# Two of seven half products read an operand's high and low part in one 512-column pass

## The chip, the cores and the metric

The kernel runs on one core of one Trainium2 chip. The metric is the device time of one execution in microseconds; times are given as the median of several runs. TensorE (PE) does the matmuls, with its weight loads shown as a row of their own (PEld); VectorE (DVE) and ScalarE (ACT) do the elementwise work; SyncE (SP) and GpSimd (POOL) issue the transfers.

## The reference

One layer of an encoder over 512 positions and 1024 channels, in fp32:

```python
x = x + 0.5 * swiglu(rms_norm(x, ffn1_norm), ffn1_w_gate, ffn1_w_up, ffn1_w_down)   # inner width 2752
h = rms_norm(x, mix_norm); u = h @ w_in
...                                              # a Fourier mixer and grouped attention, and w_out
x = x + concat([f_out, a_out]) @ w_out
x = x + 0.5 * swiglu(rms_norm(x, ffn2_norm), ffn2_w_gate, ffn2_w_up, ffn2_w_down)
return rms_norm(x, final_norm)

def swiglu(h, w_gate, w_up, w_down):
    return (silu(h @ w_gate) * (h @ w_up)) @ w_down
```

The change touches `h @ w_gate` and `h @ w_up` of both feed-forward layers.

## The kernel before

**Numbers in two parts.** TensorE works on `float32r` operands here, so each operand is held as a high part (the rounded value) and a low part (what the rounding left). A product of two operands is three matmuls that add up in one PSUM bank: high weights with high values, high weights with low values, low weights with high values. ScalarE makes a high part by a copy with a cast; VectorE makes the low part by a subtraction (`lows`, L128).

**The feed-forward layers.** The inner width is cut into 21 blocks of 128 columns (and a rest of 64). A function `ffn` runs each layer in groups of blocks: the gate and up products of a group, then the down product (`dn`) that adds this group's share to all eight output blocks. The first group of each layer is done in the plain way. From there on 35 blocks, called j (17 in the first layer, 18 in the second), are done in `seven(js, done)`, in three calls per layer: six, six and five blocks in the first layer, and six, six and six in the second. Each call is one long stretch of matmuls on TensorE, and a `dn` stretch follows it.

**Seven products in place of eight.** For a block j, the gate and up weights (1024 by 128 each) and the values (1024 by 512) form a 2 by 2 product of halves, done by Winograd's scheme with seven half products. Each half product has a weight half (`a11`, `a12`, `s1`, `s2`, `s4`, `s3`, `a22`: 512 by 128, four pieces of 128 by 128) and a half of the values (`b11`, `b21`, `t1`, `t2`, `b22`, `t3`, `t4`: 512 by 256, held in the tile `rt`). `multiply` runs it as 4 pieces times 3 matmuls of 256 columns, each into the first half of a 512-column bank. So a block has 84 passes, and a call of `seven` with six blocks has 72 passes for each block and 12 more, the `a22` product, for each block but the last; the last block's `a22` product comes a little later, between two `dn` passes.

**Which bank, and who reads it.** `step(j, w, n)` is one product and what follows. n = 0 (`a11`) writes bank r, which ScalarE copies to `p1`; n = 1 (`a12`) writes a bank of its own (named p in the profile), and VectorE adds it to `p1` into the second half of `g`; n = 3 (`s1`) writes bank q, copied to `p5`; n = 4 (`s2`) adds to r, copied to `u2`; n = 5 (`s4`) adds to q, and VectorE adds q and `u2` into the first half of `g`, which then gets its Silu on ScalarE; n = 6 (`s3`) adds to r, is copied to `u` and gets `p5`; n = 9 (`a22`, after `a12` of the next block) adds to r and ends the block. A copy has to be done before the next product adds to the same bank: `s4` waits for the copy `p5`, `s3` for the copy `u2`.

**Order.** TensorE and SyncE run in the written order. VectorE and ScalarE run each in an order that the tile scheduler works out when the program is built. `prepare(j)` makes the weight parts of the next block while the present one is multiplied.

**One pass in two pieces.** `parts_of(n)` cuts the pass with number 1 of each call of `seven` into 64 and 192 columns (`CUT = 1, P // 2`); every other pass is one piece. `product` (the plain way) has a form that reads the values in the order that `turned` gives: four columns out of each sixteen, four times; the `dn` passes are of this form, 512 columns each.

Of the kernel before, what the change touches and what calls it, by code (L numbers as in the profile page):

```python
# [13 lines left out]
P = 128  # L14
# [72 lines left out]
def encoder(ctx, tc, A, out):  # L87
# [19 lines left out]
    def bank(name):  # L107
        return pp.tile([P, S], F32, tag="bank", name=name)
# [173 lines left out]
    def ffn(norm, after, wgu, wd, wdt, groups, opening, closing):  # L282
# [6 lines left out]
        with tc.tile_pool(name=f"act{n_}", bufs=1) as ap, tc.tile_pool(name=f"sums{n_}", bufs=2) as sp:  # L289
            room(ap, 128)  # L290
            acts = ap.tile([P, PLACES * 2 * S + ROOM], F32R, name=f"at{n_}")
            at = acts[:, FRONT + LOWER : FRONT + LOWER + PLACES * 2 * S].rearrange("p (n a b) -> p n a b", a=2, b=S)
            rt = ap.tile([P, 7, 2, KH, HALF], F32R, name=f"rt{n_}")
            wt, raws = [], {}
            free, where = list(range(PLACES)), {}

# [110 lines left out]
            def seven(js, done):  # L407

                done = [done]
                banks = {}  # L410
                count = iter(range(84 * len(js)))

                def multiply(ps, wn, on, w, first):

                    (whi, wlo), (mhi, mlo) = w[wn], (part[on][:, i] for i in range(2))
                    for i in range(KH):
                        ks = slice(i * P, (i + 1) * P)
                        for o, (a, b) in enumerate(((whi, mhi), (whi, mlo), (wlo, mhi))):
                            for t in parts_of(next(count)):
                                nc.tensor.matmul(  # L420
                                    ps[:, t], a[:, ks], b[:, i, t], start=first and i == 0 and o == 0,
                                    stop=i == KH - 1 and o == 2, skip_group_check=not first,
                                )
                    give(*w.get((wn, "slots"), ()))

                def kept(ps, n, j):
                    t = sp.tile([P, HALF], F32, tag=n, name=f"{n}{n_}_{j}")
                    nc.scalar.copy(t, ps)  # L428
                    return t

                def step(j, w, n):
                    b = banks.setdefault(j, {})
                    if n == 0:
                        b["r"] = bank(f"r{n_}_{j}")[:, :HALF]
                        multiply(b["r"], "a11", "b11", w, True)
                        b["p1"] = kept(b["r"], "p1", j)
                    elif n == 1:
                        ps = bank(f"p2{n_}_{j}")[:, :HALF]
                        multiply(ps, "a12", "b21", w, True)
                        b["g"] = tp.tile([P, S], F32, tag="g", name=f"g{n_}_{j}")  # L440
                        nc.vector.tensor_tensor(out=b["g"][:, HALF:], in0=ps, in1=b["p1"], op=ALU.add)
                    elif n == 3:
                        b["q"] = bank(f"q{n_}_{j}")[:, :HALF]
                        multiply(b["q"], "s1", "t1", w, True)
                        b["p5"] = kept(b["q"], "p5", j)
                    elif n == 4:
                        multiply(b["r"], "s2", "t2", w, False)
                        b["u2"] = kept(b["r"], "u2", j)
                    elif n == 5:
                        multiply(b["q"], "s4", "b22", w, False)  # L450
                        nc.vector.tensor_tensor(out=b["g"][:, :HALF], in0=b["q"], in1=b["u2"], op=ALU.add)  # L451
                        nc.scalar.activation(b["g"], b["g"], AF.Silu)  # L452
                    elif n == 6:
                        multiply(b["r"], "s3", "t3", w, False)
                        b["u"] = tp.tile([P, S], F32, tag="u", name=f"u{n_}_{j}")
                        nc.scalar.copy(b["u"][:, :HALF], b["r"])
                        nc.vector.tensor_tensor(
                            out=b["u"][:, :HALF], in0=b["u"][:, :HALF], in1=b["p5"], op=ALU.add
                        )
                    elif n == 9:  # L460
                        multiply(b["r"], "a22", "t4", w, False)
                        u, i = b["u"], place(j)
                        h, l = at[:, i, 0], at[:, i, 1]
                        nc.scalar.copy(u[:, HALF:], b["r"])  # L464
# [1071 lines left out]
```

## Time and profile before

| | |
|---|---|
| Time, median of 3 runs | 821.32 us (820.55 to 821.43) |
| The profiled execution's own time | 820.94 us |
| Its span, first to last instruction | 818.9 us |
| TensorE busy | 812.4 us (99%), 5362 matmuls |
| VectorE busy | 637.5 us (78%), 1003 instructions |
| ScalarE busy | 483.1 us (59%), 810 instructions |
| GpSimd busy | 29.3 us (4%) |
| Transfers | 89.97 MB, 110 GB/s in the mean |

A matmul's row in the profile has a modelled end, and matmuls overlap: the 256-column matmul of `multiply` is listed with 276 ns, but one follows the other much faster. The time that a matmul takes on the engine is therefore read as a pitch: the time of a long row of equal matmuls divided by their number, from the chain of waits or from the starts in the timeline. "Idle before" names what ended an engine's idle time. Line numbers are those of the kernel before.

### The profile page before, as it was taken

The page shows a single profiled execution, that of the slowest core. Times are in us where ns is not written, and L with a number is a line of the kernel's source. Part 1 is how long each engine was busy: PE and PEld are TensorE (multiplying, and loading weights), DVE is VectorE, ACT ScalarE, POOL GpSimd, SP SyncE. Part 2 cuts the span into 40 slices and gives each one's busy share as a digit, 9 for nine tenths or more (in the row PEclk, how much of TensorE's full clock was granted, in tenths as well). Part 3 has the DMA queues.
Part 4 walks back from the last instruction along what each step waited for, and adds up shares of the span by engine and source line. Part 5 has one row for each costly group of instructions (what it writes and reads, how often), then busy time and mean ns, then how long its engine had stood idle before and what let it go on. Part 6 is the DMA issues. An engine that isn't in the chain of part 4 may idle for free.

```text
span 818.9 us, 13611 instructions
## 1 busy us (share of the span) xinstructions
PE 812.4 (99%) x5362; PEld 746.1 (91%) x5362; DVE 637.5 (78%) x1003; ACT 483.1 (59%) x810; POOL 29.3 (4%) x31
## 2 busy tenths in 40 slices
PE   9999999999999999999999999999999999999997
PEld 7889999899989998889998888899989999899987
DVE  7898896479856847799998578999945896479574
ACT  7763674257523735699998448456632673257462
POOL 0110000000000000221000001100000000000001
PEclk9999999999999999999999999999999999999999
DMA  7664322333141223342101234542232322322222
GB/s 258 174 145 179 124 93 77 124 104 142 59 151 71 90 70 116 129 147 66 65 26 52 77 112 127 123 176 108 94 122 114 127 100 69 132 104 97 69 78 103
DMA packets 31568, 89.97 MB, mean 110 GB/s; under 512 B 3728, under 2 KB 9232, under 8 KB 31504
## 3 DMA queue, kind: packets, MB, share of 16 engines
q1 hardware_dynamic: 27776, 82.61, 29.1%
q0 software_dynamic: 3008, 5.51, 3.7%
q10 hardware_dynamic: 720, 0.98, 0.3%
q8 instruction: 42, 0.69, 0.3%
q14 instruction: 22, 0.18, 0.1%
HBM read 84.24 MB, written 2.10 MB: 105 GB/s over the span
## 4 chain that ended last, share of the span: by engine, by line
PE 95%; DVE 2%; ACT 1%; POOL 1%; issue 1%; DMA 0%; POOLq 0%; DVEq 0%; ACTq 0%
PE dn L184 25%; PE r L420 23%; PE q L420 12%; PE gu L184 8%; PE mix L184 6%; PE p L420 6%; PE gu L709 3%; PE mix L1203 2%; PE mix L1169 2%; PE mix L1007 1%; PE mix L1008 1%; PE mix L1009 1%; PE mix L1066 1%; PE mix L1143 1%; PE mix L1144 1%
## 5 line engine op out<-in xcount | busy, mean ns | idle before, releaser
L420 PE MATMUL r<-rt,ring 128*128 128x256 f32 x1686 | 209.2, 276 | 0.0
L184 PE MATMUL dn<-at,ring 128*128 128x512 f32 x900 | 202.5, 380 | 0.0
L420 PEld LDWEIGHTS r<-rt,ring 128*128 128x128 f32 x1686 | 200.3, 188 | 0.8
L184 PEld LDWEIGHTS dn<-at,ring 128*128 128x128 f32 x900 | 168.0, 188 | 28.3
L420 PE MATMUL q<-rt,ring 128*128 128x256 f32 x840 | 106.6, 276 | 0.0
L128 DVE TENSOR_TENSOR ring<-s,ring 128x1024 fp32r<-128x1024 f32 x70 | 85.5, 1221 | 23.8 <-ACT ring L379 20.8
L420 PEld LDWEIGHTS q<-rt,ring 128*128 128x128 f32 x840 | 100.4, 188 | 0.0
L544 DVE SCALAR_TENSOR_TENSOR gx<-dn,gx 128x512 f32<-128x512 f32 x61 | 41.9, 688 | 67.1 <-PE dn L184 67.1
L379 ACT CAST ring<-s 128x1024 fp32r<-128x1024 f32 x70 | 73.5, 1050 | 28.3 <-PE p L420 13.7
L170 ACT CAST ring<-raw_dn 128x768 fp32r<-128x768 f32 (+3 forms) x58 | 45.3, 784 | 72.8 <-PE dn L184 61.9
L128 DVE TENSOR_TENSOR ring<-raw_dn,ring 128x768 fp32r<-128x768 f32 (+3 forms) x58 | 51.5, 892 | 5.7 <-PE r L420 4.4
L420 PE MATMUL p<-rt,ring 128*128 128x256 f32 x420 | 53.3, 276 | 0.0
L128 DVE TENSOR_TENSOR ring<-raw_g,ring 128x1024 fp32r<-128x1024 f32 x35 | 42.7, 1220 | 11.7 <-PE p L420 10.2
L420 PEld LDWEIGHTS p<-rt,ring 128*128 128x128 f32 x420 | 50.2, 188 | 0.0
L184 PE MATMUL gu<-ring 128*128 128x512 f32 x216 | 48.9, 381 | 0.0
L379 ACT CAST ring<-raw_g 128x1024 fp32r<-128x1024 f32 x35 | 36.8, 1051 | 17.2 <-DMA raw_g<-in_wgu 11.5
L184 PEld LDWEIGHTS gu<-ring 128*128 128x128 f32 x216 | 40.4, 188 | 6.9
L428 ACT COPY p<-r 128x256 f32<-128x256 f32 x35 | 12.9, 369 | 44.9 <-PE r L420 44.6
L452 ACT ACTIVATE g<-g 128x512 f32<-128x512 f32 x35 | 22.2, 633 | 23.9 <-DVE g L451 23.6
L388 ACT CAST ring<-raw_u 128x512 fp32r<-128x512 f32 x35 | 21.8, 624 | 16.0 <-PE q L420 15.7
L184 PE MATMUL mix<-near,ring 128*128 128x512 f32 x120 | 28.8, 381 | 0.0
L465 DVE TENSOR_TENSOR u<-g,u 128x512 f32<-128x512 f32 x35 | 24.0, 687 | 6.1 <-ACT u L464 6.0
(266 smaller groups left out, 1314.3 us busy)
## 6 DMA issues: line engine op xcount, KB each, us to landing
raw_g<-in_wgu SPq DMA_DIRECT2D x35, 512.0 KB, 3.8
raw_u<-in_wgu SPq DMA_DIRECT2D x35, 512.0 KB, 4.3
raw_dn<-in_wd SPq DMA_DIRECT2D x40, 384.0 KB, 3.1
raw_gu<-in_wgu SPq DMA_DIRECT2D x12, 512.0 KB, 3.7
raw_o<-in_wo SPq DMA_DIRECT2D x8, 512.0 KB, 3.5
raw_dn<-in_wd SPq DMA_DIRECT2D x8, 448.0 KB, 3.7
raw_wq<-in_wins SPq DMA_DIRECT2D x4, 512.0 KB, 3.5
raw_f<-in_winf SPq DMA_DIRECT2D x4, 512.0 KB, 3.5
```

Source lines behind the costliest of these rows:

```text
L128: nc.vector.tensor_tensor(out=lo, in0=src, in1=asf(hi), op=ALU.subtract)
L170: nc.scalar.copy(hi[:, :n, :], raw[:, :n, :])
L184: nc.tensor.matmul(ps, a, b, start=first and b is mhi and a is whi, stop=last and a is wlo)
L379: nc.scalar.copy(hi, src)
L388: nc.scalar.copy(hi, src)
L420: nc.tensor.matmul(ps[:, t], a[:, ks], b[:, i, t], start=first and i == 0 and o == 0, stop=i == KH - 1 and o == 2, skip_group_check=not first,
L452: nc.scalar.activation(b["g"], b["g"], AF.Silu)
L465: nc.vector.tensor_tensor(out=u, in0=b["g"], in1=u, op=ALU.mult)
L544: nc.vector.scalar_tensor_tensor(out=x[d][:, t], in0=ps[:, t], scalar=0.5, in1=x[d][:, t], op0=ALU.mult, op1=ALU.add)
L709: nc.tensor.matmul(turned(pss[c]), w[:, k % 2, c], turned(m[k]), start=k == 0 and m is hh and w is hi, stop=k == KD - 1 and w is lo,)
L1169: nc.tensor.transpose(pts[n][:, c * P : (c + 1) * P], prob[t, b, c][:, kc * P : (kc + 1) * P], ident)
L1203: nc.tensor.matmul(turned(outs[t, b]), w, turned(p), start=kc == 0 and i == 0, stop=kc == 3 and i == 1)
```

## The change

`a12` and `s4` get a wide form. In `rt`, the high and the low part of a piece now lie side by side (256 and 256 columns). For the two wide products, one 512-column pass in the `turned` order reads both parts with the high weights and writes both halves of the bank: high times high in the first half, high times low in the second. The low weights with the high values are a 256-column pass as before, into the first half. So the bank holds two halves that have to be added: `added` does one more addition of 256 columns on VectorE, for `g`. The other five products keep their three passes of 256 columns. The count of passes starts at 2, so no pass is cut into 64 and 192 columns in `seven` (the one in the last `dn` stretch stays).

```diff
+WIDE = ('a12', 's4')
...
-            rt = ap.tile([P, 7, 2, KH, HALF], F32R, name=f"rt{n_}")
+            rt = ap.tile([P, 7, KH, 2, HALF], F32R, name=f"rt{n_}")
...
-                        h, l = rt[:, c, 0, i], rt[:, c, 1, i]
+                        h, l = rt[:, c, i, 0], rt[:, c, i, 1]
...
-                count = iter(range(84 * len(js)))
+                count = iter(range(2, 84 * len(js)))

                 def multiply(ps, wn, on, w, first):

-                    (whi, wlo), (mhi, mlo) = w[wn], (part[on][:, i] for i in range(2))
+                    whi, wlo = w[wn]
                     for i in range(KH):
-                        ks = slice(i * P, (i + 1) * P)
-                        for o, (a, b) in enumerate(((whi, mhi), (whi, mlo), (wlo, mhi))):
-                            for t in parts_of(next(count)):
-                                nc.tensor.matmul(
-                                    ps[:, t], a[:, ks], b[:, i, t], start=first and i == 0 and o == 0,
-                                    stop=i == KH - 1 and o == 2, skip_group_check=not first,
-                                )
+                        ks, m = slice(i * P, (i + 1) * P), part[on][:, i].rearrange("p a b -> p (a b)")
+                        start, stop = first and i == 0, i == KH - 1
+                        if wn in WIDE:
+                            nc.tensor.matmul(turned(ps), whi[:, ks], turned(m), start=start, stop=False, skip_group_check=True)
+                        else:
+                            for o in range(2):
+                                for t in parts_of(next(count)):
+                                    nc.tensor.matmul(
+                                        ps[:, t], whi[:, ks], m[:, o * HALF :][:, t], start=start and o == 0, stop=False,
+                                        skip_group_check=True,
+                                    )
+                        nc.tensor.matmul(
+                            ps[:, :HALF], wlo[:, ks], m[:, :HALF], start=False, stop=stop, skip_group_check=True
+                        )
...
+                def added(out, ps, other, n):
+                    nc.vector.tensor_tensor(out=out, in0=ps[:, :HALF], in1=other, op=ALU.add)
+                    if n in WIDE:
+                        nc.vector.tensor_tensor(out=out, in0=ps[:, HALF:], in1=out, op=ALU.add)
...
                     elif n == 1:
-                        ps = bank(f"p2{n_}_{j}")[:, :HALF]
+                        ps = bank(f"p2{n_}_{j}")
                         multiply(ps, "a12", "b21", w, True)
                         b["g"] = tp.tile([P, S], F32, tag="g", name=f"g{n_}_{j}")
-                        nc.vector.tensor_tensor(out=b["g"][:, HALF:], in0=ps, in1=b["p1"], op=ALU.add)
+                        added(b["g"][:, HALF:], ps, b["p1"], "a12")
...
                     elif n == 5:
                         multiply(b["q"], "s4", "b22", w, False)
-                        nc.vector.tensor_tensor(out=b["g"][:, :HALF], in0=b["q"], in1=b["u2"], op=ALU.add)
+                        added(b["g"][:, :HALF], b["q"], b["u2"], "s4")
                         nc.scalar.activation(b["g"], b["g"], AF.Silu)
```

On TensorE, the first call of `seven` in the first layer (block 4; bank r, then bank p) begins before the change with the cut pass, after the last six passes of `dn`:

```order
L184 MATMUL dn_7_0_685<-at_128,ring 128x4x32x4 x6
L420 MATMUL r_4_712<-rt_129,ring 128x256
L420 MATMUL r_4_712<-rt_129,ring 128x64
L420 MATMUL r_4_712<-rt_129,ring 128x192
L420 MATMUL r_4_712<-rt_129,ring 128x256 x10
L420 MATMUL p_4_728<-rt_129,ring 128x256 x12
```

After the change, the last passes of the same `a11` product (bank r) and the first of `a12` (bank p) read:

```order
L425 MATMUL r_4_712<-rt_129,ring 128x256 x2
L429 MATMUL r_4_712<-rt_129,ring 128x256
L421 MATMUL p_4_727<-rt_129,ring 128x4x32x4
L429 MATMUL p_4_727<-rt_129,ring 128x256
L421 MATMUL p_4_727<-rt_129,ring 128x4x32x4
```

The twelve equal passes of bank p have become four pairs of a 512-column and a 256-column pass; the pieces of 64 and 192 are gone. In all the matmuls go from 5362 to 5076: 280 by the 70 wide products, 6 by the cuts.

On ScalarE, the scheduler works out another order, since the Silu of `g` now waits for one more addition. In the first call of `seven` in the first layer (blocks 7 to 9; `raw_dn` is a weight block of the next `dn` stretch) there stood before:

```order
L456 COPY u_7_1174<-r_7_1063 128x256
L452 ACTIVATE g_7_1091<-g_7_1091 128x512
L170 CAST ring<-raw_dn_1_1_1446 128x768
L428 COPY p_8_1198<-r_8_1185 128x256
L379 CAST ring<-raw_g_9_1179 128x1024
L464 COPY u_7_1174<-r_7_1063 128x256
L379 CAST ring<-s_0_9_1183 128x1024
L388 CAST ring<-raw_u_9_1180 128x512
L428 COPY p_8_1250<-q_8_1237 128x256
```

And now, the same copies and casts under new line numbers:

```order
L479 COPY u_7_1149<-r_7_1044 128x256
L171 CAST ring<-raw_dn_1_1_1409 128x768
L440 COPY p_8_1161<-r_8_1160 128x256
L469 ACTIVATE g_7_1068<-g_7_1068 128x512
L380 CAST ring<-raw_g_9_1154 128x1024
L440 COPY u_7_1149<-r_7_1044 128x256
L380 CAST ring<-s_0_9_1158 128x1024
L389 CAST ring<-raw_u_9_1155 128x512
L440 COPY p_8_1210<-q_8_1209 128x256
```

The Silu of block 7 has moved behind a cast and a copy; the copy `p5` of block 8 (last row), for which TensorE's `s4` product waits, stands at the same place in the queue.

More of the change, by code (lines that the diff above doesn't have):

```diff
@@ L426, in kept @@
[L426 to L429, printed above, removed]
+                        ks, m = slice(i * P, (i + 1) * P), part[on][:, i].rearrange("p a b -> p (a b)")
[9 more added lines that the diff above has]
+                                    )
@@ L431, in step, with kept, part_tile @@
+                def kept(out, ps, wide=False):
+                    nc.scalar.copy(out, ps[:, HALF:] if wide else ps[:, :HALF])
+                    if wide:
+                        nc.vector.tensor_tensor(out=out, in0=ps[:, :HALF], in1=out, op=ALU.add)
+                def part_tile(n, j):
+                    return sp.tile([P, HALF], F32, tag=n, name=f"{n}{n_}_{j}")
                 def step(j, w, n):
@@ L433, in step @@
                     if n == 0:
-                        b["r"] = bank(f"r{n_}_{j}")[:, :HALF]
+                        b["r"], b["p1"] = bank(f"r{n_}_{j}"), part_tile("p1", j)
                         multiply(b["r"], "a11", "b11", w, True)
-                        b["p1"] = kept(b["r"], "p1", j)
+                        kept(b["p1"], b["r"])
                     elif n == 1:
-                        ps = bank(f"p2{n_}_{j}")[:, :HALF]
+                        ps = bank(f"p2{n_}_{j}")
                         multiply(ps, "a12", "b21", w, True)
                         b["g"] = tp.tile([P, S], F32, tag="g", name=f"g{n_}_{j}")
-                        nc.vector.tensor_tensor(out=b["g"][:, HALF:], in0=ps, in1=b["p1"], op=ALU.add)
+                        added(b["g"][:, HALF:], ps, b["p1"], "a12")
                     elif n == 3:
-                        b["q"] = bank(f"q{n_}_{j}")[:, :HALF]
+                        b["q"], b["p5"] = bank(f"q{n_}_{j}"), part_tile("p5", j)
                         multiply(b["q"], "s1", "t1", w, True)
-                        b["p5"] = kept(b["q"], "p5", j)
+                        kept(b["p5"], b["q"])
                     elif n == 4:
                         multiply(b["r"], "s2", "t2", w, False)
-                        b["u2"] = kept(b["r"], "u2", j)
+                        b["u2"] = part_tile("u2", j)
+                        kept(b["u2"], b["r"])
                     elif n == 5:
                         multiply(b["q"], "s4", "b22", w, False)
-                        nc.vector.tensor_tensor(out=b["g"][:, :HALF], in0=b["q"], in1=b["u2"], op=ALU.add)
+                        added(b["g"][:, :HALF], b["q"], b["u2"], "s4")
                         nc.scalar.activation(b["g"], b["g"], AF.Silu)
@@ L455, in step @@
                         b["u"] = tp.tile([P, S], F32, tag="u", name=f"u{n_}_{j}")
[L456 to L459, printed above, removed]
+                        u = b["u"][:, :HALF]
+                        if "s3" in WIDE:
+                            nc.scalar.copy(b["u"], b["r"])
+                            nc.vector.tensor_tensor(out=u, in0=u, in1=b["u"][:, HALF:], op=ALU.add)
+                            nc.vector.tensor_tensor(out=u, in0=u, in1=b["p5"], op=ALU.add)
+                        else:
+                            nc.scalar.copy(u, b["r"][:, :HALF])
+                            nc.vector.tensor_tensor(out=u, in0=u, in1=b["p5"], op=ALU.add)
                     elif n == 9:
@@ L463, in step @@
                         h, l = at[:, i, 0], at[:, i, 1]
-                        nc.scalar.copy(u[:, HALF:], b["r"])
+                        kept(u[:, HALF:], b["r"], "a22" in WIDE)
                         nc.vector.tensor_tensor(out=u, in0=b["g"], in1=u, op=ALU.mult)
```

## The prediction

> **What bounds the kernel now.** I read the busy times first, then TensorE's waits, then the chain of waits for the pitch of each kind of pass, then stretches around the places where 256 and 512 columns meet. The page's first part, and all the waits of TensorE in the whole execution:
>
> ```profile
> PE 812.4 (99%) x5362; PEld 746.1 (91%) x5362; DVE 637.5 (78%) x1003; ACT 483.1 (59%) x810; POOL 29.3 (4%) x31
> PE busy L654 <- PEq L1519: 0.8, 1, 0.8
> PE mix L1143 <- DVE near L128: 0.2, 1, 0.2
> ```
>
> TensorE waits for 1.0 us of 818.9, and none of it is in the feed-forward layers. So the time there is the sum of the pitches, and an edit is worth what it does to them, unless it makes a new wait. The chain of waits gives the pitches, each row a run of equal passes (start, length, count):
>
> ```profile
> 163.10 1.49 PE r L420 x13
> 170.03 2.72 PE r L420 x24
> 218.99 3.96 PE dn L184 x18
> 224.32 27.72 PE dn L184 x126
> ```
>
> A 256-column pass takes 2.72 / 24 = 113.3 ns, a 512-column one 27.72 / 126 = 220.0 ns. Two narrow passes (226.7 ns) cost 6.7 ns more than one wide pass: a pass has a fixed part of about 6.7 ns. The first product of a call, with its pass cut in pieces, takes 1.49 us where twelve whole passes take 1.36: the cut costs 0.13 us. TensorE's clock was not throttled, and VectorE is the engine next to it (columns: length, then busy us and count of PE, PEld, DVE, ACT, POOL, then the granted clock, DMA share, GB/s):
>
> ```profile
> 162.94:218.71 55.77, 55.77 (x493) 55.77 (x492) 49.92 (x73) 35.99 (x63) 0.00 (x0) 1.00 0.30 102
> 538.17:593.95 55.78, 55.78 (x494) 55.78 (x492) 52.67 (x79) 35.27 (x62) 0.00 (x0) 1.00 0.31 112
> ```
>
> The first is a common call of `seven`, with VectorE busy 90% of it, the second the fullest one, with 94%.
>
> **Part 1: two passes become one.** 35 blocks x 2 products x 4 pieces = 280 pairs, 6.67 ns each: 280 x 6.67 = -1.87 us. [...]
>
> **Part 2: the widths now alternate.** A wide product is wide, narrow, wide, narrow: eight changes of width in a product (the one at its start included), 8 x 70 = 560, which the kernel before has only where `dn` and `seven` meet. There the first pass behind a change of width is longer. The same groups in two moments of 40 to 60 ns, each catching one change (mean ns of one), and the group of all narrow passes:
>
> ```profile
> L184 PE MATMUL dn<-at,ring 128*128 128x512 f32 x1 | 0.4, 384 | 0.0
> L184 PE MATMUL dn<-at,ring 128*128 128x512 f32 x1 | 0.4, 380 | 0.0
> L420 PE MATMUL r<-rt,ring 128*128 128x256 f32 x1 | 0.3, 279 | 0.0
> L420 PE MATMUL r<-rt,ring 128*128 128x256 f32 x1674 | 209.0, 276 | 0.0
> ```
>
> 384 against 380 for a wide one behind narrow ones, 279 against 276 for a narrow one behind wide ones: 3.5 ns in the mean. These ends are modelled, so I hold them against the clock: 18 wide and 12 narrow passes, with two changes, last from 218.99 to 224.32 = 5.33 us, and their pitches add up to 3.96 + 1.36 = 5.32. That is 0.01 us for two changes, at the limit of what a row shows, and agrees. 560 x 3.5 ns = +1.96 us. From below, the changes cost nothing (0 us); from above, see the rivals. So parts 1 and 2 together come to +0.09 us: the merge pays for its own changes of width, and no more.
>
> **Part 3: no cut.** Six calls x 0.13 = -0.78 us. The twelve narrow `a22` passes between two `dn` stretches stand behind wide passes without any cut, and the round above shows them at their usual pitch; so I take it that the first product of a call needs none either. If it did, it would have only these twelve passes to lose on before the widths change again.
>
> **Part 4: more for VectorE, and another order on ScalarE.** 70 more additions of 128x256. The rows of VectorE and ScalarE that price them, and TensorE's `s4` product (start, length):
>
> ```profile
> 183.19 0.42 DVE L457 TENSOR_TENSOR u<-u,p 128x256 f32<-128x256 f32 x1
> 183.53 0.69 DVE L394 TENSOR_TENSOR s<-raw_g,raw_u 128x512 f32<-128x512 f32 x1
> 112.15 0.64 ACT L452 ACTIVATE g<-g 128x512 f32<-128x512 f32 x1
> 112.68 0.83 ACT L170 CAST ring<-raw_dn 128x768 fp32r<-128x768 f32 x1
> 116.90 0.37 ACT L428 COPY p<-q 128x256 f32<-128x256 f32 x1
> 117.65 1.52 PE L420 MATMUL q<-rt,ring 128*128 128x256 f32 x12
> ```
>
> An addition takes 183.53 - 183.19 = 0.34 us of the queue, so a call of six blocks gets 12 x 0.34 = 4.1 us more work: 54.0 of 55.8 us in the common call, 56.8 of 55.8 in the fullest. VectorE still ends within the stretch, or 1.0 us behind it, and `dn` stretches of some 28 us, where it does less, follow; I take this as hidden. If that cover is gone, it is a rival below. On ScalarE the Silu, 112.68 - 112.15 = 0.53 us of the queue, moves behind the cast of `raw_dn` and a copy. Behind it stands the copy `p5`, for which `s4` waits: it ended at 116.90 + 0.37 = 117.27, and `s4` began at 117.65, so there is 0.38 us of room. If ScalarE stands idle where the Silu was, it is 0.53 - 0.38 = 0.15 us late. I count two such places: +0.30 us. From below: none (the cast takes the free time and nothing is late); from above: the rival again. The second addition also holds bank p or q 0.34 us longer; eight banks serve three products per block, and no wait on a bank is among TensorE's waits, so that costs nothing.
>
> **The sum.** -1.87 + 1.96 - 0.78 + 0.30 = -0.39 us. The profiled execution took 820.94 us (span 818.9 and 2.0 around it), so 820.55 for it; it lies 0.38 below the median of the runs, 821.32, against which I forecast: 821.32 - 0.39 = 820.9. 0.2% of it, about what a measurement of this kernel can tell from no change, is 1.6 us.
>
> **The rivals.** *Changes of width are free (faster).* The 3.5 ns come from modelled ends, and the clock shows 0.01 us for two. With no stall either: -1.87 - 0.78 = -2.65, so 818.7 us. Against it: both kinds of change show longer rows.
>
> *The wide passes run slow (slower).* Nowhere in the trace does a pass of the `turned` form read `rt`. And the same form has a slow state elsewhere: in the mixing part, the timeline has
>
> ```profile
> 338.70 5.14 PE L184 MATMUL mix<-ring 128*128 128x512 f32 x21
> 343.68 0.60 PE L943 MATMUL mix<-ident,kw 128*128 128x128 f32 x4
> ```
>
> (343.68 - 338.70) / 21 = 237 ns per pass, 17 more than in `dn`, at an unbroken row of passes. At that pitch the pairs cost 280 x 17 = 4.8 us more: 820.9 + 4.8 = 825.7. It decides from about 7 ns more per pass (2 us). [...]
>
> *The narrow passes behind a wide product take long to settle (slower).* In the mixing part, 24 narrow passes behind wide ones:
>
> ```profile
> 375.12 0.28 PE L1007 MATMUL mix<-ring 128*128 128x256 f32 x1
> 377.88 0.38 PE L1143 MATMUL mix<-ks,near 128*128 128x512 f32 x1
> ```
>
> 2.76 us where 24 x 113.3 are 2.72: 0.04 lost in each entry. With 70 entries 2.8 us: 823.7. Against it: `rt`'s own narrow passes behind `dn` lose less than 0.01.
>
> *VectorE or ScalarE becomes the bound (slower).* 1.0 us in the fullest call, and two late copies of 0.15 us in each of the six calls (1.8), in place of the 0.30: +2.5, so 820.9 + 2.5 = 823.4. It decides where the room of 0.38 us is used up in every call.
>
> **How the numbers follow.** My forecast, 820.9, has 0.42 and holds from 819.7 to 822.9. Free changes of width 0.22 (818.7); slow wide passes 0.12 (825.7); slow settling 0.12 (823.7); VectorE or ScalarE 0.12 (823.4). Faster by over 0.2% comes from the first rival, 0.22; slower from the other three, 0.36; within it 0.42. The range runs from a little below the free case, 818.4, to 824.7: past the second and third slower case, leaving out most of the slow wide passes (0.1) and some of the free case.
>
> **What would show it.** In the profile after: a wide product of four pairs near 4 x 340 = 1.36 us, as before (1.33 if changes are free, 1.43 with slow passes); narrow stretches at 113.3 ns from their first passes on; a call of six blocks 0.13 us shorter; VectorE near 54 us in a common call; TensorE's waits for ScalarE or VectorE inside the calls at 0.3 us in all. I am wrong if a wide product is off 1.36 us by more than 0.02, if the passes of the first product without a cut are slower than 113.3 ns, or if TensorE waits more than 1 us in the calls.

## The result, and the profile after

The changed kernel takes 825.26 us (median of 6 runs, 822.57 to 827.39) against 821.33 us for the kernel before (6 runs, 820.55 to 821.43): ratio 1.0042, 95% interval 1.0022 to 1.0063. It is slower by about 4 us, where 0.4 us less was forecast, and beyond the range (818.4 to 824.7). The traced execution of the changed kernel took 824.98 us, 822.9 of them its span, 4.0 us more than the span before.

The page's row of busy times and all the waits of TensorE, of the kernel after:

```profile
PE 814.7 (99%) x5076; PEld 738.1 (90%) x5076; DVE 660.3 (80%) x1073; ACT 484.0 (59%) x810; POOL 29.3 (4%) x31
PE dn L185 <- DVE ring L129: 1.5, 1, 1.5
PE busy L675 <- PEq L1540: 0.8, 1, 0.8
PE gu L730 <- ACT ring L716: 0.5, 1, 0.5
```

TensorE runs 286 passes fewer and is nonetheless busy 2.3 us longer. VectorE does its 70 more additions, and no wait of TensorE in the whole list lies in `seven`. What is new are longer passes in `seven`, a wait of 1.5 us in a `dn` stretch, and one of 0.5 us in the first stretch (`gu`).

**The passes.** The timeline of TensorE at the first pass of the second call of `seven` and at the `dn` pass behind the call, first of the kernel before and then of the kernel after (columns: start, length, then line, tiles and shape):

```profile
162.94 0.28 PE L420 MATMUL r<-rt,ring 128*128 128x256 f32 x1
...
218.83 0.38 PE L184 MATMUL dn<-at,ring 128*128 128x512 f32 x1
```

```profile
165.44 0.28 PE L425 MATMUL r<-rt,ring 128*128 128x256 f32 x1
...
221.68 0.39 PE L185 MATMUL dn<-at,ring 128*128 128x512 f32 x1
```

A call of six blocks took 55.89 us and takes 56.24: 0.35 more. All five such calls do, to 0.01 us; the call of five blocks goes from 46.37 to 46.76. Together +2.14 us, where the prediction's first three parts had -0.69. A wide `a12` product and the narrow one behind it, in the timeline of the kernel after:

```profile
175.04 0.39 PE L421 MATMUL p<-rt,ring 128*128 128x512 f32 x1
175.27 0.28 PE L429 MATMUL p<-rt,ring 128*128 128x256 f32 x1
...
176.30 0.29 PE L429 MATMUL p<-rt,ring 128*128 128x256 f32 x1
176.42 0.40 PE L425 MATMUL r<-rt,ring 128*128 128x256 f32 x2
...
177.80 0.39 PE L425 MATMUL q<-rt,ring 128*128 128x256 f32 x2
```

Wide product 176.42 - 175.04 = 1.38 us, the narrow one behind it 177.80 - 176.42 = 1.38; before, each took 1.36. By the trace's starts in ns, nearly all 70 wide products are alike: passes of 228, 116, 224, 123, 224, 123, 224, 122 ns, 1.384 us, and then 1.376 us for the next product until its passes are back at 113.3. That is 24 + 16 = 40 ns per wide product, 70 x 0.040 = 2.80 us; the missing cut gives back 0.78, since a first product without it takes 1.363 us, and one late pass in the call of five blocks (see the run without second additions) takes 0.11: 2.80 - 0.78 + 0.11 = 2.13, which is what the calls lost.

**The wait.** The chain of waits of the kernel after, in the second `dn` stretch (start, length, what), and VectorE's wait for these weights, before and after:

```profile
149.62 5.96 DMA raw_u<-in_wgu
155.60 0.04 DVE s L395
...
156.90 0.88 DVE ring L129
...
157.82 4.25 PE dn L185 x18
```

```profile
DVE s L394 <- DMA raw_u<-in_wgu: 0.6, 1, 0.6
```

```profile
DVE s L395 <- DMA raw_u<-in_wgu: 3.0, 1, 3.0
```

The weights of the block after next land 5.96 us after they were sent for. On VectorE the sums that read them stand ahead of the low parts of `raw_dn_6` (L129), which TensorE needs at once; the order was the same before, but there the weights came after 3.6 us. That stretch takes 29.53 us in place of 27.72: +1.81. The rest is the first stretch, up to `dn` (+0.34), and small differences in and around the mixing part (-0.29): 2.14 + 1.81 + 0.34 - 0.29 = 4.0, the whole difference.

### The profile page after: what moved, and what is told of

The parts are those of the page before. It is cut to its first block, busy times and chain, and to the rows that moved or that the text cites. A ratio compares the mean times of both kernels' runs of the same rounds, so it can differ in the third digit from the quotient of the medians.

```text
span 822.9 us, 13082 instructions
## 1 busy us (share of the span) xinstructions
PE 814.7 (99%) x5076; PEld 738.1 (90%) x5076; DVE 660.3 (80%) x1073; ACT 484.0 (59%) x810; POOL 29.3 (4%) x31
## 4 chain that ended last, share of the span: by engine, by line
PE 96%; DMA 1%; DVE 1%; ACT 1%; issue 0%; POOL 0%; POOLq 0%; DVEq 0%; ACTq 0%
PE dn L185 24%; PE r L425 16%; PE mix L185 8%; PE r L429 8%; PE gu L185 8%; PE q L429 4%; PE q L425 4%; PE q L421 4%; PE p L421 4%; PE gu L730 3%; PE p L429 2%; PE mix L1224 2%; PE mix L1190 2%; PE mix L1028 1%; PE mix L1029 1%; PE mix L1030 1%
## 5 line engine op out<-in xcount | busy, mean ns | idle before, releaser
L425 PE MATMUL r<-rt,ring 128*128 128x256 f32 x1120 | 197.0, 277 | 0.0
L425 PEld LDWEIGHTS r<-rt,ring 128*128 128x128 f32 x1120 | 170.5, 188 | 3.0
L429 PE MATMUL r<-rt,ring 128*128 128x256 f32 x560 | 155.1, 277 | 0.0
L429 PEld LDWEIGHTS r<-rt,ring 128*128 128x128 f32 x560 | 105.3, 188 | 0.0
L129 DVE TENSOR_TENSOR ring<-s,ring 128x1024 fp32r<-128x1024 f32 x70 | 85.5, 1221 | 9.4 <-ACT ring L380 8.5
L429 PE MATMUL q<-rt,ring 128*128 128x256 f32 x280 | 78.5, 280 | 0.0
L129 DVE TENSOR_TENSOR ring<-raw_dn,ring 128x768 fp32r<-128x768 f32 (+3 forms) x58 | 51.6, 892 | 5.9 <-PE r L425 4.4
L429 PEld LDWEIGHTS q<-rt,ring 128*128 128x128 f32 x280 | 52.7, 188 | 0.0
L129 DVE TENSOR_TENSOR ring<-raw_g,ring 128x1024 fp32r<-128x1024 f32 x35 | 42.7, 1221 | 11.0 <-PE p L421 9.7
L421 PE MATMUL q<-rt,ring 128*128 128x512 f32 x140 | 49.9, 386 | 0.0
L421 PE MATMUL p<-rt,ring 128*128 128x512 f32 x140 | 49.8, 385 | 0.0
L425 PE MATMUL q<-rt,ring 128*128 128x256 f32 x280 | 49.4, 277 | 0.0
L440 ACT COPY u<-r 128x256 f32<-128x256 f32 x70 | 26.1, 373 | 35.4 <-PE r L429 34.8
L425 PEld LDWEIGHTS q<-rt,ring 128*128 128x128 f32 x280 | 42.3, 188 | 0.2
```

What stands on the lines that cost most here:

```text
L129: nc.vector.tensor_tensor(out=lo, in0=src, in1=asf(hi), op=ALU.subtract)
L421: nc.tensor.matmul(turned(ps), whi[:, ks], turned(m), start=start, stop=False, skip_group_check=True)
L425: nc.tensor.matmul(ps[:, t], whi[:, ks], m[:, o * HALF :][:, t], start=start and o == 0, stop=False, skip_group_check=True,)
L429: nc.tensor.matmul(ps[:, :HALF], wlo[:, ks], m[:, :HALF], start=False, stop=stop, skip_group_check=True)
L440: nc.scalar.copy(out, ps[:, HALF:] if wide else ps[:, :HALF])
```

## The experiments

Theory A was that a change of width costs more than the prediction had it: a wide product with its neighbour lost 40 ns net of the 26.7 that four merged pairs should save, so 66.7 / 8 = 8 ns a change; theory B that the rest of the 4 us is the wait. Rivals were VectorE's added work, and, later, the place and form of the operands (theory C) and a fetch of instructions (theory D). Times are medians, and each ratio stands against the kernel before on the same chip.

### Passes, VectorE or the rest of the change?

**The changed kernel once more.** No edit.

> The changed kernel once more, unaltered. Its six executions so far lie in two groups, 822.6 (two) and 825.0 to 827.4 (four), and the traced one of the second group has a single wait of 1.5 to 1.8 us of TensorE in the dn stretch near 158 us, behind weights (raw_u) that land 6.0 us after their issue where the kernel before has 3.6. Theory A (dear changes of width): about +1.3 us over before in any execution, from wide products of 1.384 us. Theory B (the wait): the rest, 0 to 4 us, from one execution to the next, so two groups again, the lower at 822.6. Rival (the added VectorE work is the whole cost): one group, and waits spread over the calls.

Measured: 823.56 us (823.08 to 826.35, 7 runs) against 820.89, ratio 1.0033 [1.0017, 1.0049]. The calls take 56.24 us again (one of them 56.37). The traced execution (826.35) has the wait in `dn`, 2.0 us, behind weights that landed 6.46 us after their issue. The times don't fall into two groups as clearly as expected, and the kernel before has a tail too on this chip (820.33 to 823.99); e.g. the first stretch, before any `dn` pass, differs by up to 2.8 us among the traced executions of all kernels. So the steady part is the calls. Both traced executions of the change have the wait; that it is missing in the faster ones is likely, but no trace shows it.

**No wide product.** `-WIDE = ('a12', 's4')` `+WIDE = ()`.

> No wide product at all; only the new order of rt and the missing cut are left of the change. Theory A: products of 1.36 us, no narrow pass off 113.3, six cuts of 0.13 us saved: 0.8 below before, 820.5. If the new order of rt cost something by itself, narrow passes would be longer and the time above 821.3. For the wait in dn: if it comes from TensorE's smaller number of instructions, it isn't here (5,356 of them instead of 5,076); if from anything else that was changed, it may be.

Measured: 820.60 us against 820.89, ratio 0.9997 [0.9986, 1.0007], and calls of 55.76 us, all narrow passes at 113.3 ns. The new layout of `rt` costs nothing and the cut isn't needed: 0.13 us per call, as forecast. In the total the 0.78 us can't be told from no change; the lowest of the runs differ by 0.71 (819.62 against 820.33).

**No second additions.** In `added`: `-if n in WIDE:` and the `tensor_tensor` under it. The upper half of the bank is left out of the result.

> The changed kernel without the second additions of the two wide products (the upper half of the bank, high part by low part, is left out of the result). Theories A and C, by which the loss is in TensorE's pitches: calls stay at 56.24 us and the time where it is, whatever VectorE saves (4.1 us of busy time per call). Rival (VectorE's added work is the bound): a call falls by 0.35 us or more, to 55.9 or less.

A call of this kernel, from its first pass to the `dn` pass behind it, and below it the same call of the kernel after (columns: length, then busy us and count of PE, PEld, DVE, ACT, POOL, clock, DMA share, GB/s):

```profile
165.81:222.05 56.24, 56.24 (x446) 54.48 (x444) 50.06 (x73) 36.06 (x63) 0.00 (x0) 1.00 0.29 102
165.44:221.68 56.24, 56.24 (x446) 54.49 (x444) 52.82 (x84) 35.67 (x62) 0.00 (x0) 1.00 0.30 97
```

VectorE has 50.06 us of work instead of 52.82, and the call is as long as before the edit: 56.24 us. (The time, 825.86, one run, holds a first stretch 1.8 us longer.) VectorE's load is no part of the loss in these calls. Only the call of five blocks gets shorter, 46.64 for 46.76: there one `s4` pass of the kernel after came 0.11 us late, behind the copy `p5`.

### What sets the length of a pass

**The wide passes first, then the narrow ones**, in each wide product:

```
-for i in range(KH):
+for i, low in [(i, low) for low in range(2) for i in range(KH)] if wn in WIDE else ...:
```

> In a wide product the four wide passes come first, then the four narrow ones: two changes of width per product instead of eight, the same passes, the same additions. Theory A: 4 x 220 + 4 x 113.3 = 1.333 us and some 0.03 for the entry and the change, 1.36 instead of 1.384: 70 x 0.024 = 1.7 us less than the changed kernel, 820.9 where the wait in dn is absent. Rival (wide passes over rt are 224 to 228 ns and narrow ones with their bank 122 by themselves, whatever the order): product 1.38 us, no gain, 822.6. Rival (VectorE's additions): no gain either.

Measured: 826.99 us against 820.89, ratio 1.0079 [1.0060, 1.0099]: slower still, with a quarter of the changes of width. Its timeline at `a12` and behind it:

```profile
173.18 1.07 PE L421 MATMUL p<-rt,ring 128*128 128x512 f32 x4
174.09 0.63 PE L430 MATMUL p<-rt,ring 128*128 128x256 f32 x4
174.55 0.40 PE L426 MATMUL r<-rt,ring 128*128 128x256 f32 x2
...
175.97 0.40 PE L426 MATMUL q<-rt,ring 128*128 128x256 f32 x2
...
177.38 0.40 PE L426 MATMUL r<-rt,ring 128*128 128x256 f32 x2
```

The four wide passes take 0.91 us where 4 x 220 are 0.88, and the two narrow products behind them take 1.42 and 1.41 us: 117.7 ns per pass for 24 passes in a row, with nothing changing among them. Behind `s4` they are at 113.3 at once. So the price isn't one per change, and theory A falls: in this run the same narrow passes had two steady pitches, 117.7 ns behind `a12` and 113.3 behind `s4`.

**The same with a cut behind each wide product:**

```
-for t in parts_of(next(count)):
+for t in parts_of(1 if i == 0 and o == 1 and after_wide[0] else 0):
```

> The kernel with the four wide passes first and then the four narrow ones, where the narrow passes kept 117.7 ns for whole products behind each wide one; now the second pass of the product behind a wide one is in pieces of 64 and 192 columns. If the slower pitch is a state that the stream of passes keeps until its rhythm is broken, the narrow passes return to 113.3 ns behind the pieces, and a call falls from 56.83 us by most of 0.9 us, less 12 x 0.13 for the cuts (about 57.5). If the slower pitch belongs to the passes themselves, it stays and the cuts only add: about 58.4 us.

```profile
167.34 0.63 PE L430 MATMUL p<-rt,ring 128*128 128x256 f32 x4
167.81 0.48 PE L426 MATMUL q<-rt,ring 128*128 128x256 f32 x3
...
169.31 0.39 PE L426 MATMUL r<-rt,ring 128*128 128x256 f32 x2
...
170.67 0.39 PE L421 MATMUL q<-rt,ring 128*128 128x512 f32 x1
```

The product with the pieces takes 1.50 us, and the next one 1.36: back at 113.3 ns. A call takes 57.68 us, near the 57.5 expected of a state that can be broken. The slow pitch behaved here as a state that the pass in pieces ended: 113.3 ns behind it, where 117.7 stood without it. At 0.14 us (1.50 for 1.36) the cut costs more than the slow pitch that it ends here: a call is 0.85 us longer than with the wide passes first and no cuts.

**Contiguous wide passes.** `-nc.tensor.matmul(turned(ps), whi[:, ks], turned(m), ...` `+nc.tensor.matmul(ps, whi[:, ks], m, ...`.

> The wide passes of seven read rt and write their bank contiguously, 512 columns in a row, instead of in the turned order; sizes, places and the alternation with narrow passes stay. Theory A (the change of width itself is dear): the wide product stays at 1.384 us and a call at 56.24 us. Theory C (the turned form at rt's place is what is dear: rt lies at another distance from the next weights than every other operand that is read turned): 4 x (220.0 + 113.3) = 1.333 us, a call of six blocks 55.76 - 12 x 0.027 = 55.44 us, and with that 818.3 + 6 x (55.44 - 55.89) + 2 = about 818 us, below before.

```profile
176.09 0.40 PE L421 MATMUL p<-rt,ring 128*128 128x512 f32 x1
176.33 0.28 PE L429 MATMUL p<-rt,ring 128*128 128x256 f32 x1
176.45 0.40 PE L425 MATMUL r<-rt,ring 128*128 128x256 f32 x2
...
177.86 0.40 PE L425 MATMUL q<-rt,ring 128*128 128x256 f32 x2
```

Theory C's number was wrong, and in sign: 832.98 us against 821.19, ratio 1.0148 [1.0132, 1.0165]. Wide passes take 235 ns, and all narrow ones of the call, from the first wide product on, 117.7. The turned form was the better one here: with it the stream comes back to 113.3 ns.

**Other places.** First the wait's test in its first form: it has one small tile more in a pool, which moves the operands behind it, `rt` and `at`, by 64 bytes relative to the weights.

> The changed kernel, with VectorE's sums that read raw_u held behind the low parts of raw_dn_6 in each dn stretch (through a factor of one that is made from those low parts: one tiny instruction more per stretch). A late raw_u then holds nothing that TensorE needs in dn. Theory B: one group at 822.6, within 0.5 us, and no wait of TensorE near 158 us, even where raw_u lands late. Rival (something else makes the slower group): still executions of 825 to 827.

```profile
172.01 0.40 PE L432 MATMUL r<-rt,ring 128*128 128x256 f32 x2
...
172.73 0.40 PE L432 MATMUL r<-rt,ring 128*128 128x256 f32 x2
```

Six passes in 0.72 us, 120 ns each; a `dn` stretch takes 28.76 us in place of 27.72, and the kernel 845.06 us against 820.89, ratio 1.0290 [1.0276, 1.0304]. It told nothing of the wait, but of the passes: the same edit without the move takes 823.45 us (below), so the place of the operands alone is worth some 21 us here. Then `rt` alone, 16 bytes further on (`rt = rt_tile[:, 4 : ...]`):

> The changed kernel with rt 16 bytes further on, so that its turned wide passes lie at the distance from the next weights at which all other turned passes of the program lie, and its narrow contiguous ones do not. Theory C: wide passes fall to 220 ns, narrow ones become longer than 113.3 (some 118 to 120, as in the run in which a shift of all places made them 120). Theory A: wide passes stay at 224 ns. The call of six blocks is then longer than 56.24 us by Theory C, because most passes are narrow.

Measured: 835.46 us (one run), narrow passes of 118.8 and wide ones of 228 ns in the mean, calls of 57.99 us. As theory C had it, the narrow contiguous passes get slower; the wide ones, against it, don't get faster. Then three of the seven operands there, and all passes that read them turned (`form = turned if on[0] == "b" else ...`):

> The three operands b11, b22, b21 lie 16 bytes further on in rt, where every other turned operand of the program lies, and all passes that read them (the products a11, a12 and s4, narrow ones too) are turned; the four sums' operands and their narrow contiguous passes stay where they are. The alternation of widths in a12 and s4 stays as in the change. Theory C (form and place together decide whether TensorE keeps its short pitch): no pass leaves 113.3 and 220.0 but for some 4 ns at a change, the wide product takes 1.34 to 1.35 us, and a call 55.76 - 12 x (0.01 to 0.02) = 55.5 to 55.6 us: some 6 x 0.3 = 1.8 us below before, 819.0 to 819.5. Theory A (any change of width costs 8 ns): product 1.384 us, call 56.24 us. If narrow turned passes are slow by themselves, the a11 products show it.

Measured: 826.88 us against 820.81, ratio 1.0076 [1.0062, 1.0089]; wide passes of 220 to 236 ns, calls of 56.90. Not what theory C forecast. And all of `rt` there, with all passes turned:

> All of rt lies 16 bytes further on and every pass of seven is turned, narrow or wide. Theory C: all passes at 113.3 and 220.0, calls of 55.5 to 55.6 us. If narrow turned passes have a longer pitch, all calls are longer, by 12 x 36 times that pitch's excess.

```profile
168.81 0.38 PE L425 MATMUL q<-rt,ring 128*128 128x512 f32 x1
169.03 0.28 PE L433 MATMUL q<-rt,ring 128*128 128x256 f32 x1
...
170.14 0.39 PE L429 MATMUL r<-rt,ring 128*128 128x256 f32 x2
```

This wide product runs in 170.14 - 168.81 = 1.33 us, 220 and 113.5 ns in turn: the merge as it was meant, with eight changes of width that cost nothing. Half of the 70 do so, 29 of the `a12` products and 6 of the `s4` ones. But nearly all others take 1.371 and the narrow turned passes 115.5 in the mean, so a call takes 56.47 us (824.24, one run). Place and form mattered in these runs, then (where they were moved, narrow passes took 115.5, 118.8 and 120 ns, for 113.3), but no rule that foretells the pitch showed.

**The narrow pass ahead of the wide one** in each pair:

> As the change, but in each pair the narrow pass comes before the wide one. The number of changes of width, the forms and the places are the same. If a change of width has a fixed price, products stay at 1.384 us; if the order in which TensorE enters the alternation decides, they are anywhere from 1.335 (the best of the alternating products so far) to 1.414 us (the contiguous ones).

Wide product 1.375 us and the next one 1.385, calls of 56.24 us, 821.98 us (one run, without the wait). As in the change.

**Eight wide passes in a row.** `WIDE = ('s4', 's3')`, `s4`'s narrow passes first and `s3`'s last. The high part by low part of `s3` is missing from the second half of the output.

> Wide are s4 and s3, which follow each other, with s4's narrow passes first and s3's last, so that eight wide passes stand in one row: two changes of width per two wide products. Places and forms as in the change. If changes of width were what costs (8 ns each), the two take 2 x 1.333 + 0.02 = 2.69 us and a call 55.76 - 6 x 0.03 = 55.6 us. If TensorE's rhythm decides, which settles behind some passes, the eight wide passes show 227 to 233 ns before 220, and the narrow ones behind them may keep 117.7: a call of 56 to 57 us.

```profile
168.69 1.07 PE L421 MATMUL q<-rt,ring 128*128 128x512 f32 x4
169.60 1.07 PE L421 MATMUL r<-rt,ring 128*128 128x512 f32 x4
170.51 0.63 PE L430 MATMUL r<-rt,ring 128*128 128x256 f32 x4
170.98 0.39 PE L426 MATMUL r<-rt,ring 128*128 128x256 f32 x2
```

The wide ones take (170.51 - 168.69) / 8 = 228 ns in the mean, the last four no less than the first, so no change of width is to blame for them; of the narrow ones behind, four take 116 to 119, and the rest 113.3. Calls of 55.92 us, 821.09 us (one run). And with all of `rt` moved and turned:

> The same order, with all of rt 16 bytes further on and every pass of seven turned, where one of the two wide products per block ran at 220.0 and 113.5 ns. The narrow turned passes there had 115.5 in the mean, so a call of 4 or 5 narrow products per block stays above 56 us; the eight wide passes should run at 220 ns, and the two wide products take 2.68 to 2.70 us.

With the same part missing: eight wide passes in 1.769 us, in most rows 220 from the fourth on, as expected; but the narrow turned ones hold the call at 56.00 us (821.91, one run). Last, both findings together, with nothing left out of the result: `a12` and the block before's `a22` wide, in one row, their operands moved and turned, the other five products as they were.

> A version that takes up what the runs showed. Wide are a12 and the block before's a22, which follow each other; a12's narrow passes come first, a22's last, so that eight wide passes stand in a row; b21 and t4, which they read, lie 16 bytes further on and are read turned in all their passes; the five other products stay contiguous at the old place. If place, form and row make the pitch: narrow passes 113.3, wide ones 220 to 222 in the mean, the turned narrow ones 115: the two products 2.69 us in place of 2.72, a call of six blocks 55.76 - 6 x 0.03 = 55.6 us, and 819.0 to 819.5 us, 1.3 to 1.8 below before. If the entry from contiguous passes upsets the rhythm again (as where the three b operands were moved), the wide ones take 228 us/1000 and the call 55.9 to 56.2 us: 821 to 823.

```profile
172.59 0.62 PE L437 MATMUL p<-rt,ring 128*128 128x256 f32 x4
173.05 1.06 PE L428 MATMUL p<-rt,ring 128*128 128x512 f32 x4
...
174.83 0.61 PE L437 MATMUL r<-rt,ring 128*128 128x256 f32 x4
175.28 0.40 PE L433 MATMUL q<-rt,ring 128*128 128x256 f32 x2
```

The wide row takes 1.78 us and its two products 175.28 - 172.59 = 2.69, 0.03 less than before, and the narrow product behind takes 1.389, 0.03 more. Most calls take 55.78 us, what they take with no wide product at all, two of them 0.2 more: 821.97 us against 820.64, ratio 1.0016 [1.0008, 1.0025]. I found no version that beats both kernels by more than the runs can tell.

| kernel | wide product | narrow one behind it | call of six blocks |
|---|---|---|---|
| before / no wide product | - | 1.360 | 55.89 / 55.76 |
| after | 1.384 | 1.376 | 56.24 |
| wide passes first, `a12` / `s4` | 1.379 / 1.367 | 1.413 / 1.360 | 56.83 |
| contiguous | 1.414 | 1.413 | 57.89 |
| all turned and moved, `a12` / `s4` | 1.335 / 1.371 | 1.371 / 1.402 | 56.47 |

(Medians over the 35 or 70 products of a traced execution, us.)

### The wait in dn

**VectorE's sums held back**, behind the low parts of `raw_dn_6`, through a factor of one that is made from these and lies in an unused place:

```
+nc.vector.tensor_scalar(out=held[0], in0=asf(wlo[:, 0, :1]), scalar1=0.0, scalar2=1.0, ...)
+nc.vector.scalar_tensor_tensor(out=out, in0=a, scalar=one, in1=b, op0=ALU.mult, op1=op)
```

> As the run of this kind before (VectorE's sums that read raw_u held behind the low parts of raw_dn_6), but with the factor of one in an unused place, so that no other operand moves: there every place moved by 64 bytes and nearly every pass got slower. Theory B (the wait in dn): calls at 56.24 us, no wait of TensorE near 158 us, dn stretches of 27.72 us each, and times within 822.3 to 823.5 but for what the first stretch varies; median some 0.5 to 1.5 below the changed kernel's 823.6 on the same chip. Rival: a wait there in spite of it.

Measured: 823.45 us (822.89 to 825.84) against 821.19, ratio 1.0031 [1.0020, 1.0043]. The traced execution has no wait in `dn` and stretches of 27.72 us. But `raw_u` landed after 4.0 us there, which may have been early enough by itself, and the median is no lower than the repeat's: it fits theory B and proves little.

**Twelve tiny passes at the start**, behind the nine with which TensorE begins (427 ns each in the kernel after), and nothing else:

```
+for _ in range(12):
+    nc.tensor.matmul(busy[:, :64], one[0], one[1][:, :64], start=True, stop=True)
```

> The changed kernel with 12 tiny passes of 64 columns more behind the nine that warm TensorE up at the start: 24 instructions of TensorE more ahead of everything else, and nothing else. Theory D (the late raw_u comes from a 16 KB fetch of instructions that, with fewer TensorE instructions ahead of it, falls on the moment in which the weights raw_g and raw_u are sent for): the fetch comes 24 x 113 ns = 2.7 us earlier in relation to that moment, as in the run with cuts behind the wide products (fetch 2.5 us ahead of raw_g's issue, landing 3.6 us), so raw_u lands 3.6 us after its issue and there is no wait in dn: 27.72 us for that stretch. Rival (landings of 4 to 6.5 us belong to the kernels with wide products for another reason, or are chance): 4 us or more again, with a wait of up to 4 us. The start costs up to 1.7 us more.

SyncE's queue at the two loads in question, and the row of the DMA queues in which a 16 KB packet of instructions shows, first of the kernel after (146 to 147.4 us for the packet), then of this one (142.5 to 144.5 us), with VectorE's wait:

```profile
146.04 1.36 SPq L372 DMA_DIRECT2D raw_g<-in_wgu  x1
149.62 0.33 SPq L372 DMA_DIRECT2D raw_u<-in_wgu  x1
q8 instruction: 1, 0.02, 4.1%
```

```profile
145.13 0.42 SPq L372 DMA_DIRECT2D raw_g<-in_wgu  x1
148.70 0.33 SPq L372 DMA_DIRECT2D raw_u<-in_wgu  x1
q8 instruction: 1, 0.02, 3.0%
DVE s L395 <- DMA raw_u<-in_wgu: 0.6, 1, 0.6
```

In the kernel after the packet starts at 146.11, in the very moment in which `raw_g` is sent for, whose issue takes 1.36 us in place of 0.42. Here it starts at 143.27, 1.86 us ahead; `raw_u` lands after 3.6 us, and the wait is gone. The time is 822.51 us (822.08 to 823.42, 10 runs) against 820.65, ratio 1.0024 [1.0015, 1.0034], with a spread of 1.3 us where the changed kernel had 4.8 and 3.3: what is left is 1.9 us, about the 2.1 of the calls. In all 18 traces the landing of `raw_u` goes with the packet: 3.5 to 3.6 us where it lies over 1.5 us ahead of `raw_g`'s issue or far behind it (in the kernel before at 161.55), and 3.9 to 6.5 where it falls within 0.5 us of that issue. So theory D fits the wait: one edit that moved the packet took it away, and no trace speaks against it. Whose instructions the packet carries, and why it also lies early with the narrow pass first and with `s4` and `s3` wide, which have as many instructions of TensorE as the change, stays open.

## Why the prediction was wrong, point by point

**Part 1** (280 x 6.67 ns less) was right as arithmetic: the products that ran at their best pitches, half of those with all passes turned, took 1.335 us, 0.025 less than before.

**Part 2 is the step that failed.** It took 3.5 ns for each of 560 changes of width, from two rows at single changes, and +1.96 us. The calls' +2.14, less the 0.11 of the late pass, needs 2.03 + 1.87 + 0.78 = 4.68 us, 8.4 ns each. By the starts it lies in the wide passes (225 ns in the mean, 5 more than 220), in the narrow ones between them (121, 8 more than 113.3) and in the product behind (16 ns): 280 x 5 + 280 x 7.7 + 70 x 16 = 4.7 us. And the term wasn't only too small. A price per change was the wrong kind of term: with the same widths the runs gave anything from no loss at all (half of the wide products, all turned) to narrow passes that stay slow for 24 in a row (wide ones first). The two rows came from places where a long row of equal passes lies on each side. In a wide product no two neighbours are equal, and its passes stay at 224 and 123 ns in turn. Why the stream takes one pitch or another is not shown. The rival of narrow passes that take long to settle had the mechanism nearest to this, with +2.8 us for 70 entries; the runs gave 70 x 0.040 = 2.80 net of the saving. That the numbers are equal is luck: only 16 ns per entry lie in the narrow product behind, where the rival had 40, and 24 in the wide one.

**The rival of slow wide passes** had 237 ns from the mixing part. By the starts in that row the first pass takes 320 ns and the other 20 take 233, so its price was 280 x 13 = 3.7 us, not 4.8. As changed, the wide passes took 224 to 228 ns; the contiguous form took 235. That its 825.7 us lies near the measured 825.26 is luck too: some 1.4 us of the loss are the wide passes', and 1.81 of the traced execution's are a wait in `dn`. That an operand's place can cost showed where the operands moved by 64 bytes: 120 for 113.3 ns, and 28.76 for 27.72 us in `dn`.

**Part 3** was right: 0.13 us per call, -0.78, and in the first product only the first pass, with 116 ns, is off 113.3.

**Part 4** was right that VectorE stays hidden, also in the fullest call: without the additions the calls of six blocks are as long. Of the 0.30 us for ScalarE's other order, 0.11 showed, in one call.

**What no part had** is the wait in `dn`: +1.81 us in the traced execution. The prediction followed the order of each engine and its load, and not when a load that comes just in time (0.6 us of wait on VectorE, in a row that it could have read) would come late.

## What to carry to other kernels

Count a merge of passes by the pitch of the whole sequence that results, not by a sum over passes and changes: two widths in turn were a sequence of their own here (224 and 123 ns, where 220 and 113.3 had been counted), and such a pitch has to be seen before the saving (6.7 ns of 113 here) is booked. Where an in-order engine has a load's consumer ahead of something that the bounding engine needs at once, look at the slack of that load in the trace; a change that touches neither the load nor its consumer can use it up, as here, where VectorE's wait for `raw_u` went from 0.6 to 3.0 us.

## What the hardware showed that was not expected

TensorE's narrow passes had two steady pitches for the same instruction, 113.3 and 117.7 ns; with the wide passes first the stream kept the slow one behind `a12` for all 36 narrow passes up to the next wide product, and where a pass was cut in pieces it came back to the fast one behind it. Turned wide passes ran at 220 ns in `dn` and at 233 in a row of the mixing part.

In the repeat a `dn` stretch lost about twice TensorE's wait in it: the wait of 2.0 us was followed by a lower granted clock (windows of 2 us behind it; the value behind POOL's is the clock):

```profile
157.60:159.60 2.00, 2.00 (x5) 1.61 (x6) 1.97 (x4) 0.00 (x0) 0.00 (x0) 0.52 0.50 143
159.60:161.60 2.00, 2.00 (x8) 1.56 (x7) 0.74 (x1) 0.00 (x0) 0.00 (x0) 0.63 0.29 119
161.60:163.60 2.00, 2.00 (x11) 1.70 (x10) 0.52 (x1) 0.00 (x0) 0.00 (x0) 1.00 0.00 0
```

0.52 and then 0.63 of full speed in the 4 us behind the wait (in the chain of waits, the first five passes behind it take 2.46 us, where nine take 2.27 behind the other trace's wait), so that the stretch took 3.94 us more, with 2.0 of wait. Behind the wait of 1.5 us in the other trace the clock stayed at 1.00. Why it fell once and not the other time is not shown.
